# Seven products in place of eight in a feed-forward's first multiplication, with their sums on gpsimd, ScalarE and VectorE

## The chip, the cores and the metric

The kernel runs on one core of one Trainium2 chip, as one program. Its time is the device time of one execution in microseconds (us); runs are compared by their median. Engines are called as the profile calls them: PE (TensorE matmuls), PEld (its weight loads), DVE (VectorE), ACT (ScalarE), POOL (GpSimd) and SP (SyncE, which only issues DMAs here).

## What is computed

The reference runs two trunk layers over 640 tokens of width 1024: 512 latent tokens and 128 context tokens, each group with its own modulation vectors. A layer is a feed-forward, a token mixing and a second feed-forward, each behind an RMSNorm that is shifted and scaled, and each added to x with a gate:

```python
def swiglu_ffn(h, w_in, w_out):
    gate, up = jnp.split(h @ w_in, 2, axis=-1)
    return (jax.nn.silu(gate) * up) @ w_out

x = x + 0.5 * g1 * swiglu_ffn(modulate(rmsnorm(x, ...), sh1, sc1), ffn1_w_in, ffn1_w_out)
mix, ctx_state = token_mixing(modulate(rmsnorm(x, ...), sh2, sc2), ...)
x = x + g2 * mix
x = x + 0.5 * g3 * swiglu_ffn(modulate(rmsnorm(x, ...), sh3, sc3), ffn2_w_in, ffn2_w_out)
```

The hidden width is 2816, that is 22 tiles of 128. The vectors sh, sc and g are `silu(cond) @ w_ada + b_ada`, 72 tiles a layer.

## The kernel before

Tokens lie in the free dimension, features on the partitions. They are cut into half A (384 tokens) and half B (256). A feed-forward goes through its 22 hidden tiles, called units, in four blocks of 5, 5, 6 and 6 (`BLOCKS`). A unit has a gate tile and an up tile, each a sum over eight 128-feature tiles of its input. After a block's units come its out tasks: for each of eight output tiles and each half, a sum over the block's hidden tiles, added to x by `accumulate` on DVE.

Every float32 product is made of three matmuls on a high and a low part (`mm3`, lines 365 to 367), called a triple here:

```python
nc.tensor.matmul(out, hi, rhs_hi, start=start, stop=False)
nc.tensor.matmul(out, hi, rhs_lo, start=False, stop=False)
nc.tensor.matmul(out, lo, rhs_hi, start=False, stop=stop)
self.clock(MM3[rhs_hi.shape[-1]])
```

So each operand is split: ACT copies the high part (line 191) and DVE subtracts it from the source to get the low part (line 192, `split_h`). Weights come by SP's DMAs in pieces of 128x1024 and are split ahead of their use. In a unit, ACT works out silu of the gate (line 610), DVE multiplies it with the up tile out of PSUM (line 619), and the product is split into `hid`.

The order of instructions on each engine is the order in which the program is written out. A clock of the matrix work (`self.clock`, which counts the planned us of each triple) says when a piece of weight is split and when a step of background work is put in. Two kinds of background work run beside feed-forwards: `ada` (line 260), which makes modulation vectors by two 128x1024 multiply-and-sum instructions on DVE for each tile, and `ssm_build`, which makes the tables of a layer's state-space scan, in eight sets, on DVE, POOL, PE and ACT, beside each layer's first feed-forward. `ada` has 48 tiles beside the first feed-forward of layer 0 (8 of them 4.5 planned us apart, the others 7.0), 56 beside its second (8 at 4.5, then 6.5), 24 beside the first of layer 1 (10.0), and none beside the last. The first two units of the whole program are worked out beside the opening (`lead_task`).

## Time and profile before

| | us |
|---|---|
| median of 3 runs | 2525.57 |
| the runs | 2521.89 to 2526.12 |
| span of the profiled execution, first to last instruction | 2522.3 |
| PE busy | 2466.4 |
| DVE busy | 1555.2 |
| ACT busy | 812.4 |
| POOL busy | 680.9 |

The profiled execution has no time of its own beside its span; the span lies within the three runs. Busy times count instructions from their start to their end, with waits inside an instruction. Matmuls are pipelined, so the time of one matmul is longer than the distance from it to the next.

### The profile page before, as it was taken

The numbers are of one execution on the slowest core, as the hardware profiler recorded it, in microseconds if no ns is written. First come the engines' busy times: TensorE is split into PE (matmuls) and PEld (weight loads), VectorE is DVE, ScalarE is ACT, GpSimd is POOL, SyncE is SP. The second block draws the span as 40 slices with busy tenths as digits, with TensorE's granted clock in tenths as the row PEclk, the third lists the DMA queues.
The fourth block names the chain that finished last, engine by engine and source line by source line (L and its number), as shares of the span: only waits on it lengthen the run. The fifth ranks groups of instructions, "written<-read, shape, count | busy, mean of one in ns | idle before, by whom it ended". The sixth has DMA issues, their size and how long they took to land.

```text
span 2522.3 us, 44229 instructions
## 1 busy us (share of the span) xinstructions
PE 2466.4 (98%) x17428; PEld 2408.2 (95%) x17428; DVE 1555.2 (62%) x3293; ACT 812.4 (32%) x1689; POOL 680.9 (27%) x1520
## 2 busy tenths in 40 slices
PE   6999999999999999999999999999999999999999
PEld 5999999998988999999999999999998889999999
DVE  7798777557566776666568675534685764343332
ACT  5322222254444422222242222223545452222121
POOL 5105765623342000000020566551253320000000
PEclk8999999999999999999999999999999999999999
DMA  6445454325341344443324344332444212222222
GB/s 229 144 147 170 159 168 164 109 110 148 121 129 46 127 172 142 151 148 144 117 86 144 134 150 151 105 98 74 143 149 122 82 54 91 74 85 67 83 68 67
DMA packets 102115, 307.29 MB, mean 122 GB/s; under 512 B 21666, under 2 KB 24834, under 8 KB 101524
## 3 DMA queue, kind: packets, MB, share of 16 engines
q1 hardware_dynamic: 86548, 254.92, 29.8%
q0 software_dynamic: 15360, 49.56, 6.2%
q8 instruction: 137, 2.24, 0.4%
q14 instruction: 70, 0.57, 0.1%
HBM read 281.78 MB, written 23.17 MB: 121 GB/s over the span
## 4 chain that ended last, share of the span: by engine, by line
PE 87%; DVE 5%; issue 3%; ACT 2%; POOL 1%; DMA 1%; SPq 0%; DVEq 0%; POOLq 0%; ACTq 0%
PE mm L365 26%; PE mm L367 26%; PE mm L366 26%; PE mm L1389 1%; PE mm L1390 1%; PE mm L1391 1%; DVE aj L449 1%; DVE w L192 1%; PE sA L1258 1%; PE sB L1280 1%; PE mm L1227 1%; DMA T<-dT 0%; DVE H L541 0%; PE sB L1093 0%; PE sA L909 0%
## 5 line engine op out<-in xcount | busy, mean ns | idle before, releaser
L365 PE MATMUL mm<-H,w 128*128 128x384 f32 (+1 forms) x3248 | 1021.3, 314 | 9.5 <-ACT H L536 5.6
L366 PE MATMUL mm<-H,w 128*128 128x384 f32 (+1 forms) x3248 | 1011.9, 312 | 12.3 <-DVE H L541 9.3
L367 PE MATMUL mm<-H,w 128*128 128x384 f32 (+1 forms) x3248 | 1011.3, 311 | 0.0
L365 PEld LDWEIGHTS mm<-H,w 128*128 128x128 f32 x3248 | 615.0, 189 | 21.9 <-issue 13.8
L366 PEld LDWEIGHTS mm<-H,w 128*128 128x128 f32 x3248 | 615.1, 189 | 15.5 <-DVE H L541 11.1
L367 PEld LDWEIGHTS mm<-H,w 128*128 128x128 f32 x3248 | 614.7, 189 | 1.1 <-DVE w L192 1.1
L192 DVE TENSOR_TENSOR w<-r,w 128x1024 fp32r<-128x1024 f32 (+2 forms) x354 | 395.5, 1119 | 243.7 <-ACT w L191 242.3
L365 PE MATMUL mm<-hid,w 128*128 128x384 f32 (+1 forms) x1408 | 434.4, 309 | 0.0
L367 PE MATMUL mm<-hid,w 128*128 128x384 f32 (+1 forms) x1408 | 433.5, 308 | 0.0
L366 PE MATMUL mm<-hid,w 128*128 128x384 f32 (+1 forms) x1408 | 432.9, 307 | 0.0
L191 ACT ACTIVATE w<-r 128x1024 fp32r<-128x1024 f32 (+2 forms) x354 | 337.8, 956 | 289.8 <-PE mm L367 232.5
L260 DVE SCALAR_TENSOR_TENSOR aj<-ar,sbc 128x1024 bf16<-128x1024 f32 x256 | 317.4, 1240 | 36.4 <-DMA ar<-w_ada 32.4
L395 DVE SCALAR_TENSOR_TENSOR x<-mm,mod,x 128x128 f32<-128x128 f32 (+1 forms) x480 | 194.0, 434 | 183.7 <-PE mm L367 183.0
L365 PEld LDWEIGHTS mm<-hid,w 128*128 128x128 f32 x1408 | 264.1, 188 | 1.0 <-issue 1.0
L366 PEld LDWEIGHTS mm<-hid,w 128*128 128x128 f32 x1408 | 264.7, 188 | 0.0
L367 PEld LDWEIGHTS mm<-hid,w 128*128 128x128 f32 x1408 | 264.5, 188 | 0.0
L191 ACT ACTIVATE hid<-sg 128x384 fp32r<-128x384 f32 (+1 forms) x176 | 82.9, 471 | 550.4 <-DVE sg L619 534.5
L295 POOL TENSOR_TENSOR acc<-acc,sq 128x384 f32<-128x384 f32 (+1 forms) x60 | 53.7, 895 | 604.8 <-ACT sq L293 604.1
L619 DVE TENSOR_TENSOR sg<-sg,mm 128x256 f32<-128x256 f32 (+1 forms) x161 | 78.1, 485 | 212.0 <-PE mm L367 211.9
L610 ACT ACTIVATE sg<-mm 128x256 f32<-128x256 f32 (+1 forms) x161 | 70.0, 435 | 329.7 <-PE mm L367 329.7
L192 DVE TENSOR_TENSOR hid<-sg,hid 128x384 fp32r<-128x384 f32 (+1 forms) x176 | 89.2, 507 | 94.6 <-ACT hid L191 94.6
L1389 PE MATMUL mm<-w,H 128*128 128x256 f32 x480 | 143.1, 298 | 0.0
(329 smaller groups left out, 2642.2 us busy)
## 6 DMA issues: line engine op xcount, KB each, us to landing
ar<-w_ada SPq DMA_DIRECT2D x128, 512.0 KB, 4.5
r<-f1i SPq DMA_DIRECT2D x88, 512.0 KB, 3.4
r<-f0i SPq DMA_DIRECT2D x86, 512.0 KB, 3.5
r<-f0o SPq DMA_DIRECT2D x32, 384.0 KB, 3.1
r<-wqkv SPq DMA_DIRECT2D x24, 512.0 KB, 3.5
r<-f1o SPq DMA_DIRECT2D x32, 384.0 KB, 3.0
r<-f0o SPq DMA_DIRECT2D x32, 320.0 KB, 2.9
r<-f1o SPq DMA_DIRECT2D x32, 320.0 KB, 2.9
```

The lines of the kernel that those rows point to most:

```text
L191: self.nc.scalar.activation(hi, src, AF.Copy)
L192: self.nc.vector.tensor_tensor(lo, src, hi.bitcast(F32), op=ALU.subtract)
L260: nc.vector.scalar_tensor_tensor(jk, r, 1.0, self.sbc[:, c, :], op0=ALU.mult, op1=ALU.mult, accum_out=m[:, c, j * KD + k:j * KD + k + 1])
L295: eng.tensor_tensor(self.acc[X], self.acc[X], q, op=ALU.add)
L365: nc.tensor.matmul(out, hi, rhs_hi, start=start, stop=False)
L366: nc.tensor.matmul(out, hi, rhs_lo, start=False, stop=False)
L367: nc.tensor.matmul(out, lo, rhs_hi, start=False, stop=stop)
L395: nc.vector.scalar_tensor_tensor(self.x[:, m, r0:r1], p[:, r0 - s:r1 - s], self.mod[l][:, c, g * KD + m:g * KD + m + 1], self.x[:, m, r0:r ...
L449: v.scalar_tensor_tensor(jk, r, 1.0, self.sbc[:, c, :], op0=ALU.mult, op1=ALU.mult, accum_out=m[:, c, j:j + 1])
L610: nc.scalar.activation(sg[:, :e - s], p[:, :e - s], AF.Silu)
L619: nc.vector.tensor_tensor(sg[:, :e - s], sg[:, :e - s], p[:, :e - s], op=ALU.mult)
L1389: nc.tensor.matmul(p[:, :256], H[:, 0, k, ts], wh, start=k == 0, stop=False)
```

## The change

The halves are 320 tokens each. In all units but the program's first two, the products of the unit's weights with the input are taken as those of two matrices of 2 by 2 pieces: the input is cut into A and B by tokens and into its first and last four feature tiles, the weights into gate and up by columns and into the same feature halves. Seven products of such pieces, of four triples each (p1 to p7 in the code), take the place of eight. For that

- four sums of weight pieces a unit are made on POOL (`take`, 128x512 each), and seven weight pieces a unit are split instead of four pieces' worth (128x512 each; `high` on ACT, `low` on DVE);
- sums of input pieces (`x_sums`) are made once for a feed-forward, after the norm of half B, on DVE, POOL and ACT, and split;
- products that are shared are accumulated in PSUM on top of one another, and ACT copies what a bank holds midway (the prefix) to SBUF, three copies a unit;
- DVE adds or subtracts a prefix out of PSUM three times a unit, and four more combining operations of 128x320 (`tt`) go to POOL, or to DVE in the last unit of a block.

The first feed-forwards have six blocks (4, 4, 4, 4, 3, 3 units), the second ones four (6, 6, 5, 5). The out tasks and the token mixing have the same products as before. Weights are loaded in pieces of 128x512 into 24 numbered buffers, at most three sums exist at once (`NSUM`), a sum may be written out up to 13.0 planned us ahead of its use and a high part up to 9.0 (`LEAD`). Where a norm precedes, the products p1 and p2 of four units, which read half A alone, are done first (`EARLY`).

```diff
-HALF = {"A": (0, 384), "B": (384, 640)}
-RANGES = {"A": ((0, 384, 0),), "B": ((384, 512, 0), (512, 640, 1))}
-TILES = {"A": (0, 1, 2), "B": (3, 4)}
-BLOCKS = ((0, 5), (5, 5), (10, 6), (16, 6))
+HT = 320
+HALF = {"A": (0, HT), "B": (HT, 2 * HT)}
+RANGES = {"A": ((0, 320, 0),), "B": ((320, 512, 0), (512, 640, 1))}
+SEGS = {"A": ((0, 0), (128, 0), (192, 64)), "B": ((320, 0), (448, 0), (512, 64))}
+BLOCKS = (((0, 4), (4, 4), (8, 4), (12, 4), (16, 3), (19, 3)), ((0, 6), (6, 6), (12, 5), (17, 5)))
+EARLY = 4
...
-LEAD, LEAD_HOT, DMA_LAG, SPLIT_GAP = 24.0, 4.5, 3.5, 2.0
-MM3 = {384: 0.489, 256: 0.327}
+LEAD, LEAD_HOT, DMA_LAG = (13.0, 9.0), (7.0, 4.5), 3.5
+SUM_GAP, HIGH_GAP, SUM_TO_HIGH, HIGH_TO_LOW = 1.3, 0.7, 1.4, 0.6
+NW, NRAW, NSUM = 24, 7, 3
+MM3 = {320: 0.41, 256: 0.327}
...
+        def take():
+            c = order[st["a"]]
+            n, x, y = self.ops[c]
+            st["a"] += 1
+            t_sum[c] = self.T
+            if y:
+                total[c] = new((c, "t"), F32)
+                nc.gpsimd.tensor_tensor(total[c][:, :n], source(x, n), source(y, n), op=ALU.add)
+                st["sum"] = self.T
+                read(x)
...
+            if st["h"] < st["a"] and len(free) >= 2:
+                c = order[st["h"]]
+                if self.T - st["high"] >= HIGH_GAP and due(c, lead[1]) and \
+                        self.T - t_sum[c] >= (SUM_TO_HIGH if self.ops[c][2] else 0.0):
+                    high()
+            if st["a"] < len(order):
+                c = order[st["a"]]
+                if due(c, lead[0]) and (not self.ops[c][2] or
+                                        self.T - st["sum"] >= SUM_GAP and len(total) < NSUM and len(free) > 2) and \
+                        all(x is None or x[0] == "o" or x[1] in raw and self.T - when[x[1]] >= DMA_LAG
+                            for x in self.ops[c][1:]):
+                    take()
...
+    def x_sums(self, k, r12, r22):
...
+        v.tensor_tensor(t1, h11, r12, op=ALU.subtract)
+        g.tensor_tensor(t3, r12, r22, op=ALU.subtract)
+        v.tensor_tensor(t1, t1, l11, op=ALU.add)
+        v.tensor_tensor(t2, r22, t1, op=ALU.add)
+        g.tensor_tensor(t4, h21, t2, op=ALU.subtract)
+        g.tensor_tensor(t4, t4, l21, op=ALU.add)
...
+        def high(u, X, src):
+            hid[u, X] = [new((u, X, i), F32R) for i in range(2)]
+            nc.scalar.activation(hid[u, X][0], tmp[src], AF.Copy)
+        def low(u, X, src):
+            a, b = hid[u, X]
+            v.tensor_tensor(b, tmp[src], a.bitcast(F32), op=ALU.subtract)
+            drop(src)
...
+        def p1(w, u):
+            bank["a", u] = self.ps()[:, :HT]
+            self.product(bank["a", u], w, "11", True)
+            nc.scalar.activation(temp((u, "p")), bank["a", u], AF.Copy)
+        def p2(w, u):
+            p = bank.pop(("a", u))
+            self.product(p, w, "21", False)
+            nc.scalar.activation(temp((u, "a")), p, AF.Silu)
+        def p5(w, u):
+            bank["c", u] = self.ps()[:, :HT]
+            self.product(bank["c", u], w, "t1", True)
+            nc.scalar.activation(temp((u, "c")), bank["c", u], AF.Copy)
+        def p6(w, u):
+            bank["b", u] = self.ps()[:, :HT]
+            self.product(bank["b", u], w, "t2", True)
+            nc.scalar.activation(temp((u, "b")), bank["b", u], AF.Copy)
+        def steps(gap, *fns):
+            for n, fn in enumerate(fns):
+                self.later(gap * (n + 1), fn)
+        def tt(u, out, a, b, op):
+            (v if u in ends else nc.gpsimd).tensor_tensor(out, a, b, op=op)
+        def p3(w, u):
+            p = bank.pop(("c", u))
+            self.product(p, w, "22", False)
+            s, sg = temp((u, "s")), tmp[u, "b"]
+            v.tensor_tensor(s, p, tmp[u, "p"], op=ALU.add)
+            def gate():
+                tt(u, sg, s, sg, ALU.subtract)
+                drop((u, "s"))
+            steps(2 - (u in ends), gate, lambda: nc.scalar.activation(sg, sg, AF.Silu))
+        def p7(w, u):
+            self.product(bank["b", u], w, "t3", False)
+            s, a, b = temp((u, "s")), tmp[u, "b"], tmp[u, "c"]
+            v.tensor_tensor(s, bank["b", u], tmp[u, "p"], op=ALU.subtract)
+            def sub():
+                tt(u, b, s, b, ALU.subtract)
+                drop((u, "s"))
+            def mult():
+                tt(u, b, a, b, ALU.mult)
+                drop((u, "b"))
+            steps(2 - (u in ends), sub, mult, lambda: high(u, "B", (u, "c")), lambda: low(u, "B", (u, "c")))
+        def p4(w, u):
+            p = bank.pop(("b", u))
+            self.product(p, w, "t4", False)
+            a, b = tmp[u, "a"], tmp[u, "p"]
+            v.tensor_tensor(b, p, b, op=ALU.subtract)
+            def mult():
+                tt(u, b, a, b, ALU.mult)
+                drop((u, "a"))
+            if u in ends:
+                mult()
+                high(u, "A", (u, "p"))
+                self.later(2, lambda: low(u, "A", (u, "p")))
+            else:
+                steps(2, mult, lambda: high(u, "A", (u, "p")), lambda: low(u, "A", (u, "p")))
...
+        def units(us, early):
+            for u in early[:3], early[3:]:
+                if u:
+                    items.extend(early_task(u))
+            for n, u in enumerate(us):
+                if u not in early:
+                    items.append(task(p1, u, "11"))
+                items.append(task(p5, u, "s1"))
+                if n:
+                    items.append(task(p4, us[n - 1], "22"))
+                items.append(task(p6, u, "s2"))
+                if u not in early:
+                    items.append(task(p2, u, "12"))
+                items.append(task(p3, u, "s4"))
+                items.append(task(p7, u, "s3"))
+            items.append(task(p4, us[-1], "22"))
...
+            self.ops[op("s1")] = (512, r["p0"], r["p1"])
+            self.ops[op("s2")] = (512, ("o", op("s1")), r["g0"])
+            self.ops[op("s4")] = (512, ("o", op("s2")), r["g1"])
+            self.ops[op("s3")] = (512, r["g0"], r["p0"])
...
+            if lead and b == 0:
+                items.append(lead_task(us[:2]))
+                items += lead_rest(us[1])
+                items.append(("call", lambda: self.norms.update(B=self.spawn(self.all_x_sums(), 0.0, True))))
+                units(us[2:], us[2:])
+            else:
+                units(us, us[:n_early] if b == 0 else [])
```

What this does to DVE's queue in a middle unit of the last feed-forward: before, six rows are one unit (L192 of `w` is the low part of a weight piece, L619 the product with the up tile, L192 of `hid` the low part of the unit's result, for half A and half B).

```order
L192 TENSOR_TENSOR w_25880<-r_25762,w_25880 128x1024
L192 TENSOR_TENSOR w_25912<-r_25794,w_25912 128x1024
L619 TENSOR_TENSOR sg_25894<-sg_25894,mm_25896 128x384
L192 TENSOR_TENSOR hid_25742<-sg_25894,hid_25742 128x384
L619 TENSOR_TENSOR sg_25954<-sg_25954,mm_25956 128x256
L192 TENSOR_TENSOR hid_25808<-sg_25954,hid_25808 128x256
```

Of the change, the twelve rows of one unit on DVE (L220 is the low part of a weight piece, L889, L900 and L916 combine a PSUM bank, `mm`, with a prefix, L852 is the low part of a result).

```order
L220 TENSOR_TENSOR w_31032<-w_30978,w_31031 128x512
L220 TENSOR_TENSOR w_31051<-w_30751,w_31050 128x512
L852 TENSOR_TENSOR hid_31057<-hid_30837,hid_31056 128x320
L220 TENSOR_TENSOR w_31077<-w_31023,w_31076 128x512
L889 TENSOR_TENSOR hid_31106<-mm_30996,hid_30994 128x320
L220 TENSOR_TENSOR w_31101<-w_30933,w_31100 128x512
L900 TENSOR_TENSOR hid_31128<-mm_31038,hid_30994 128x320
L220 TENSOR_TENSOR w_31122<-w_31067,w_31121 128x512
L220 TENSOR_TENSOR w_31143<-w_31088,w_31142 128x512
L852 TENSOR_TENSOR hid_31160<-hid_31017,hid_31159 128x320
L220 TENSOR_TENSOR w_31166<-w_30908,w_31165 128x512
L916 TENSOR_TENSOR hid_30994<-mm_31038,hid_30994 128x320
```

The two long rows on weights have become seven of half the width, and the two products three with PSUM. POOL has nothing to do in the units of the last feed-forward of the kernel before; of the change, these eight rows on POOL belong to one unit of the last feed-forward (L199 adds two weight pieces, L883 is a combining operation).

```order
L199 TENSOR_TENSOR w_30910<-w_30866,w_30776 128x512
L199 TENSOR_TENSOR w_30931<-w_30621,w_30641 128x512
L883 TENSOR_TENSOR hid_30902<-hid_30949,hid_30902 128x320
L199 TENSOR_TENSOR w_30978<-w_30798,w_30908 128x512
L883 TENSOR_TENSOR hid_30860<-hid_30971,hid_30860 128x320
L883 TENSOR_TENSOR hid_30860<-hid_30902,hid_30860 128x320
L199 TENSOR_TENSOR w_31023<-w_30978,w_30778 128x512
L883 TENSOR_TENSOR hid_30837<-hid_30925,hid_30837 128x320
```

POOL thus has eight instructions a unit, each with two operands in SBUF, mixed from two chains. In layer 0's first feed-forward, a set of the scan's tables begins on POOL before with six rows one after the other (`EP` and `tp` are parts of a table).

```order
L728 TENSOR_TENSOR EP_2247<-Bb_2215,PW_1570 128x256
L729 TENSOR_TENSOR tp_2217<-Bb_2215,PW_1570 128x256
L730 TENSOR_TENSOR EP_2247<-EP_2247,tp_2217 128x256
L731 TENSOR_TENSOR tp_2217<-Bb_2215,PW_1570 128x256
L732 TENSOR_TENSOR EP_2247<-Bb_2215,PW_1570 128x256
L736 TENSOR_TENSOR EP_2247<-EP_2247,tp_2217 128x256
```

Of the change, rows of the same kind stand between weight sums and combining operations of the units, in one queue.

```order
L199 TENSOR_TENSOR w_4110<-w_4050,w_3946 128x512
L1107 TENSOR_TENSOR EP_4090<-EP_4090,tp_4057 128x256
L1108 TENSOR_TENSOR tp_4057<-Bb_4055,PW_1920 128x256
L199 TENSOR_TENSOR w_4137<-w_3743,w_3771 128x512
L1110 TENSOR_TENSOR EP_4090<-Bb_4055,PW_1920 128x256
L1111 TENSOR_TENSOR EP_4090<-EP_4090,tp_4057 128x256
L883 TENSOR_TENSOR hid_4102<-hid_4155,hid_4102 128x320
L199 TENSOR_TENSOR w_4186<-w_3975,w_4108 128x512
L883 TENSOR_TENSOR hid_4044<-hid_4179,hid_4044 128x320
L883 TENSOR_TENSOR hid_4044<-hid_4102,hid_4044 128x320
L199 TENSOR_TENSOR w_4242<-w_4186,w_3948 128x512
```

## Rows read from the trace of the kernel before

**Rows 1.** The page: busy totals, and 40 slices of DVE and POOL in tenths.

```profile
PE 2466.4 (98%) x17428; PEld 2408.2 (95%) x17428; DVE 1555.2 (62%) x3293; ACT 812.4 (32%) x1689; POOL 680.9 (27%) x1520
...
DVE  7798777557566776666568675534685764343332
...
POOL 5105765623342000000020566551253320000000
```

**Rows 2.** The page: chain of waits that ended last, by engine.

```profile
PE 87%; DVE 5%; issue 3%; ACT 2%; POOL 1%; DMA 1%; SPq 0%; DVEq 0%; POOLq 0%; ACTq 0%
```

**Rows 3.** Timeline of PE in a unit: start us, us, engine, line, tile, shape.

```profile
299.84 0.28 PE L366 MATMUL mm<-H,w 128*128 128x256 f32 x1
...
301.85 0.34 PE L365 MATMUL mm<-H,w 128*128 128x384 f32 x1
...
308.55 0.34 PE L367 MATMUL mm<-H,w 128*128 128x384 f32 x1
```

**Rows 4.** Groups by line and shape: count | busy us, mean ns | idle before.

```profile
L260 DVE SCALAR_TENSOR_TENSOR aj<-ar,sbc 128x1024 bf16<-128x1024 f32 x256 | 317.4, 1240 | 36.4 <-DMA ar<-w_ada 32.4 <-ACT sbc L252 2.7
...
L192 DVE TENSOR_TENSOR w<-r,w 128x640 fp32r<-128x640 f32 x64 | 53.5, 836 | 34.8 <-ACT w L191 34.2
...
L192 DVE TENSOR_TENSOR hid<-sg,hid 128x384 fp32r<-128x384 f32 x88 | 50.1, 569 | 52.1 <-ACT hid L191 52.1
L191 ACT ACTIVATE w<-r 128x640 fp32r<-128x640 f32 x64 | 46.6, 729 | 30.4 <-PE mm L367 30.4
L191 ACT ACTIVATE hid<-sg 128x384 fp32r<-128x384 f32 x88 | 46.2, 525 | 300.6 <-DVE sg L619 296.0 <-DVE sg L634 4.5
...
L192 DVE TENSOR_TENSOR hid<-sg,hid 128x256 fp32r<-128x256 f32 x88 | 39.1, 444 | 42.6 <-ACT hid L191 42.6
...
L295 POOL TENSOR_TENSOR acc<-acc,sq 128x384 f32<-128x384 f32 x30 | 30.5, 1016 | 538.2 <-ACT sq L293 538.0
...
L295 POOL TENSOR_TENSOR acc<-acc,sq 128x256 f32<-128x256 f32 x30 | 23.3, 775 | 66.6 <-ACT sq L293 66.1
```

**Rows 5.** Timeline: POOL alone at 216 us; DVE and POOL at 450 us.

```profile
216.33 0.21 POOL L728 TENSOR_TENSOR T<-T 128x14 f32<-128x14 f32 x1
...
450.30 1.22 DVE L192 TENSOR_TENSOR w<-r,w 128x1024 fp32r<-128x1024 f32 x1
...
450.40 0.19 PEld L367 LDWEIGHTS mm<-H,w 128*128 128x128 f32 x1
```

**Rows 6.** Timeline at 304.8 us, DVE and POOL.

```profile
304.77 0.73 POOL L730 TENSOR_TENSOR EP<-EP,tp 128x256 f32<-128x256 f32 x1
304.78 1.81 DVE L192 TENSOR_TENSOR w<-r,w 128x1024 fp32r<-128x1024 f32 x1
...
305.58 1.49 POOL L731 TENSOR_TENSOR tp<-Bb,PW 128x256 f32<-128x256 f32 x1
```

**Rows 7.** Timeline at 1661.6 us: POOL beside a DVE instruction that reads PSUM.

```profile
1661.60 0.83 POOL L736 TENSOR_TENSOR EP<-EP,tp 128x256 f32<-128x256 f32 x1
...
1661.76 0.54 DVE L619 TENSOR_TENSOR sg<-sg,mm 128x384 f32<-128x384 f32 x1
```

**Rows 8.** Windows: length, busy us (instructions) of each engine, PE clock, DMA share.

```profile
200.00:500.00 300.00, 300.00 (x2082) 296.60 (x2081) 219.42 (x394) 75.59 (x127) 198.57 (x505) 1.00 0.47 156
1400.00:1700.00 300.00, 300.00 (x2074) 296.58 (x2074) 177.99 (x328) 74.34 (x122) 175.68 (x502) 1.00 0.38 127
2250.00:2300.00 50.00, 50.00 (x338) 50.00 (x337) 17.89 (x28) 11.00 (x16) 0.00 (x0) 1.00 0.23 81
1250.00:1300.00 50.00, 48.96 (x333) 48.47 (x332) 27.54 (x67) 18.33 (x33) 13.84 (x15) 1.00 0.26 95
2050.00:2100.00 50.00, 48.24 (x314) 47.72 (x313) 29.18 (x68) 24.43 (x51) 5.86 (x7) 0.97 0.21 72
575.00:580.00 5.00, 2.63 (x16) 2.27 (x14) 0.57 (x1) 1.66 (x4) 0.00 (x0) 1.00 0.48 187
580.00:585.00 5.00, 4.75 (x37) 4.47 (x38) 4.83 (x14) 2.94 (x8) 0.00 (x0) 0.71 0.57 171
```

More of the change, by code (lines that the diff above doesn't have):

```diff
@@ L104, in run @@
                     last[c] = i
-        W = self.NW
-        raws, tiles, when = {}, {}, {}
-        st = {"d": 0, "s": 0, "x": 0, "i": 0, "t": self.T}
+        place = {c: j for j, c in enumerate(order)}
+        rorder, users, sums = [], {}, {}
+        for c in order:
+            for x in self.ops[c][1:]:
+                if x and x[0] == "r":
+                    if x[1] not in users:
+                        users[x[1]] = 0
+                        rorder.append(x[1])
+                    users[x[1]] += 1
+                elif x:
+                    sums.setdefault(x[1], []).append(c)
@@ new lines, in read, with over @@
+        def read(x):
+            if x[0] == "r":
+                users[x[1]] -= 1
+                if not users[x[1]]:
+                    raw.pop(x[1])
+                    free.append(slot.pop(x[1]))
+                    dma()
+        def over(c):
+            if c in total and place[c] < st["l"] and all(place[d] < st["a"] for d in sums.get(c, ())):
+                total.pop(c)
+                free.append(slot.pop((c, "t")))
+                dma()
+        def take():
[8 more added lines that the diff above has]
+                read(x)
+                read(y)
+                if x[0] == "o":
+                    over(x[1])
@@ new lines, in high, with low @@
+        def high():
+            c = order[st["h"]]
+            n, x, y = self.ops[c]
+            src = source(("o", c) if y else x, n)
+            pair[c] = new((c, 0), F32R), new((c, 1), F32R)
+            nc.scalar.activation(pair[c][0][:, :n], src, AF.Copy)
+            t_high[c] = st["high"] = self.T
+            st["h"] += 1
+        def low():
+            c = order[st["l"]]
+            n, x, y = self.ops[c]
+            src = source(("o", c) if y else x, n)
+            hi, lo = pair[c]
+            nc.vector.tensor_tensor(lo[:, :n], src, hi[:, :n].bitcast(F32), op=ALU.subtract)
+            st["l"] += 1
+            if y:
+                over(c)
+            else:
+                read(x)
@@ new lines, in due, with splitter @@
+        def due(c, lead):
+            return begin[first[c]] - (self.T - t0) <= lead
+        def splitter():
+            if self.dlimit is not None:
+                return
+            lead = LEAD_HOT if self.hot else LEAD
+            if st["l"] < st["h"] and self.T - t_high[order[st["l"]]] >= HIGH_TO_LOW:
+                low()
+            if st["h"] < st["a"] and len(free) >= 2:
+                c = order[st["h"]]
+                if self.T - st["high"] >= HIGH_GAP and due(c, lead[1]) and \
[8 more added lines that the diff above has]
+                    take()
@@ L142, in run, with have @@
+        def have(ops):
+            dma()
+            while any(place[c] >= st["l"] for c in ops):
+                if st["l"] < st["h"]:
+                    low()
+                elif st["h"] < st["a"]:
+                    high()
+                else:
+                    take()
+            return [pair[c] for c in ops]
+        self.dma, self.splitter, self.get = dma, splitter, have
         for i, it in enumerate(items):
-            st["i"] = i
             if it[0] == "call":
@@ L558, in opening @@
             if k:
[L559 to L560 removed]
+                low(k)
+            yield k, w
         assert not todo and next(by_pool, "end") == "end"
```

671 lines of the change are left out of this document (390 added, 281 removed).

## The prediction

> **What bounds the kernel now.** I read the page's totals first, then the chain of waits, then stretches. PE is busy for 98% of the span [rows 1], and 87% of the chain that ended last is PE [rows 2], so only fewer or shorter matmuls, or a new wait of PE, move the end. The timeline of PE gives the price: 17 matmuls of 256 tokens take 301.85 - 299.84 = 2.01 us, 0.118 each, and 38 of 384 tokens take 308.55 - 301.85 = 6.70 us, 0.176 each [rows 3], so 0.46 ns a token, 0.147 us for 320 and 0.442 for a triple. POOL is idle for whole slices and DVE is busy 62% [rows 1]; both look like room for the sums. What matters is whether the room of the two is one room, and that takes the timelines below.
>
> **What it removes.** Each of 86 units has 28 triples for 32, so 344 x 0.442 = 152 us less of PE. In all, a unit falls from 32 x 0.442 = 14.14 us to 28 x 0.442 = 12.37; the out tasks (22 x 16 x 0.442 = 156 us a feed-forward) stay. The profiled span of 2522.3 would become 2370 if nothing else moved. The median of the runs lies 3.3 us above that span, which I add at the end.
>
> **What it adds on ACT and elsewhere.** From [rows 4], ACT's copy of 640 columns takes 729 ns and of 384 takes 525, hence 627 for 512 and about 470 for 320. A unit has seven of the first and seven of the second kind (three prefixes, two silus, two high parts): 7.7 us of 12.37, beside PE. DVE's extra gated adds (two more blocks in each first feed-forward) fall into out tasks, where nothing else is dense. Twice as many DMAs of half the size carry about the same bytes, at a DMA share near 0.23 to 0.47 [rows 8]. I cost these at nothing; the cover is PE's own time, and it goes if ACT has to wait for a sum or a combining operation of POOL, since ACT's queue is in order and the next prefix copy stands behind.
>
> **What it adds on POOL and DVE: one room, not two.** At 450.30 us DVE starts a low part of 1024 columns, two operands in SBUF, 1.22 us long. POOL's instruction of 14 columns starts 0.10 later and lasts 1.19 where it takes 0.21 alone [rows 5]: it got through from 450.40 + 1.19 - 0.21 = 451.38 on. DVE kept it out for 1.08 us, its own duration less 0.14. The other way, at 304.77, POOL's 0.73 us instruction is under way, DVE's low part starts 0.01 later and lasts 1.81, 0.59 too long, and POOL's next one in turn lasts 1.49 [rows 6]: POOL kept DVE out for its duration less 0.13. A DVE instruction with PSUM as one operand ran at its 0.54 us beside POOL [rows 7]. So sums and combining operations on POOL, and low parts and `ada` on DVE, take turns, and their turns add up.
>
> The turns of a middle unit: POOL's add takes 1016 ns at 384 columns and 775 at 256 [rows 4], by the line 1257 at 512 and 896 at 320; less 0.13, four of 1.13 and four of 0.77 are 7.6 us. DVE's low part takes 836 ns at 640, 569 at 384 and 444 at 256 [rows 4], so 702 at 512 and 507 at 320; less 0.14, seven of 0.56 and two of 0.37 are 4.66. Sum 12.26 us, against PE's 12.37: full, with nothing beside it. Beside `ada`, each tile is two turns of 1.24 - 0.14, and 1.08 by [rows 5], so 2.16 us; a unit is 28 x 0.41 = 11.48 planned us, hence 1.64 tiles at a pace of 7.0, 1.77 at 6.5, 1.15 at 10.0: the unit's turns become 15.8, 16.1 and 14.7 us. A set of the scan's tables: POOL is busy 198.6 us with 505 instructions for eight sets [rows 8], 24.8 a set, waits and DMA issues in it. Less 505 x 0.13 that is 16.6; by a small one's share (0.08 of 0.21, [rows 5]) it is 9.4. I take 14, DVE's part in it, between the two. Eight sets beside the last 14 units of a first feed-forward and their out tasks (14 x 12.37 + 14 x 7.07 = 272 us, 173 of it units) put 0.36 of a set beside a unit, 5.1 us (3.4 by the low bound).
>
> What of that reaches PE: weights are split 9.0 planned us ahead, 9.7 real (0.442 for 0.41). A block loses its units times (turns - 12.37) less that lead, and the out tasks, in which POOL rests, bring the lead back. Turns never follow one another without a gap, since either queue also waits for data; [rows 6] shows a hand-over without any, so I add 5%, near that end.
> - First feed-forward, layer 0: the second block 4 x (16.6 - 12.37) - 9.7 = 7; the next two, with tables, 4 x (21.9 - 12.37) - 9.7 = 28 each; then 3 units 19, and 8 without `ada`; 10 for the input sums at the start (below). Sum 100.
> - Second, layer 0: 6 x (16.9 - 12.37) - 9.7 = 17.5, twice, 13 twice for five units, and 5 for the first eight tiles' faster pace. Sum 66.
> - First, layer 1 (`ada` ends about two thirds through): 3, 3, 24, 24, 8, 8. Sum 70.
> - Second, layer 1: 6 x 0.5 = 3, within the lead. Sum 0.
> - Starts of the last three: before, PE is idle 1 to 2 us there [rows 8]. Four input sums, each four turns on POOL (0.77) and six on DVE (0.37), are 21 us, to be done before p5 and p6 can end, with the norm of half B ahead of them; p1 and p2 of four units give PE 32 x 0.442 = 14. I take 9 each, 27 (bounds 13 and 40).
>
> Sum 263 us against 152 saved: 2522.3 - 152 + 263 + 3.3 = 2637. With no gaps, tables at 3.4 a unit and starts at 13, the same sums give 60 + 48 + 27 + 13 = 148, so 2522.
>
> The Trainium skill, "SBUF — State Buffer", section "Who interferes with whom", states that a DVE instruction with two SBUF inputs and a GpSimd instruction that reads SBUF exclude each other for the whole instruction, and that the other fully blocks. On the exclusion the trace agrees; taken with whole durations, which these rows shorten by 0.13 to 0.14 us, the rule gives 2826 us, the second rival below, in place of 2637.
>
> **The rivals.**
> *The turns fit (faster).* If POOL and DVE use the out tasks for the units' work, only a whole feed-forward's turns count: units, out weights' low parts (24 us), input sums (21), `ada`, tables (9.4 a set) against PE's 428 us (410 for layer 0's first, without its lead units). Layer 0 first: 245 + 24 + 23 + 104 + 75 = 471, 61 over; layer 0 second 270 + 24 + 21 + 121 = 436, 8 over; layer 1 first 270 + 24 + 21 + 52 + 75 = 442, 14 over; the last none. With 13 for starts, 2522.3 - 152 + 96 + 3.3 = 2470. For it speaks that DVE is at 18 of 50 us without `ada` and POOL at 0 [rows 8]; against it, that the queues are in order and at most three sums exist. It decides from a lead of about 25 us instead of 9.7.
> *Each instruction keeps the other out for its whole duration (much slower).* A unit's turns are then 4 x 1257 + 4 x 896 + 7 x 702 + 2 x 507 ns = 14.5 us, 18.6 to 18.9 beside `ada`, and a table set 19.8, 7.1 a unit. The same sums give 160 + 110 + 134 + 8 + 40 = 452, so 2826. Towards it also works that PE, after idling 2.4 of 5 us at 575, had a granted clock of 0.71 in the next 5 us [rows 8]: each stall may cost a second time. Against it speak [rows 5, 6].
> *No change to measure.* The low bound, 2522, lies there, but only by a balance of unlike sizes.
>
> **How the numbers follow.** My forecast (2531 to 2725) has 0.57, the turns that fit 0.21, whole durations or worse 0.19, a balance within 0.2% (5 us, about what a measurement of this kernel can tell) 0.03. Faster 0.21, same 0.03, slower 0.76. The range reaches to the first rival's 2455, of whose spread down to PE's bound (2400) it leaves out a third, and to 2750 towards the second, which leaves out two thirds of that one: about 0.8 inside. The forecast's own range is 2531 to 2725.
>
> **What would show it.** Right: PE's matmuls of the units keep 0.147 us, and PE gets waits for DVE's low parts (`w`) or ACT's copies that were absent; POOL's adds of 512 columns last well above 1.26 us in the mean, and DVE's low parts above 0.70; the units of layer 1's second feed-forward pass at about 12.4 us, those beside `ada` at 15 or more. Wrong: PE busy at 98% again with a span near 2400, or waits of PE that end with PE's own PSUM banks or with DMAs.

## The result, and the profile after

The changed kernel takes 2969.55 us in the median of four runs, 2525.03 before: 1.176 times as long, with a 95% interval of 1.174 to 1.178. Slower was forecast, but at 2637 us, with a range that ended at 2750. The profiled execution has a span of 2960.9 us at a mean granted clock of 0.921 (2522.3 at 0.992 before). All that follows goes by that span, so 438.6 us more where the forecast had 111 (263 less 152): 328 short.

The page's busy times, and its slices for three engines and the clock, against [rows 1]:

```profile
PE 2493.5 (84%) x16420; PEld 2388.6 (81%) x16420; DVE 2239.4 (76%) x4224; ACT 1120.6 (38%) x2613; POOL 1576.2 (53%) x2192
...
PE   6678788785999958898986888879889997899999
...
DVE  7899778865656688989886887877757576757766
...
POOL 5434777776334373636344557787753434734632
PEclk8899889897999979999997999989989998899999
```

PE is no longer the engine that is always busy, and no other engine is busy all the time either: DVE 76%, POOL 53%. Two engines that are half and three quarters busy can still be the limit if they work in turns. The chain of waits accounts for too little of this span to be of use, so the next view is PE's waits, by whom it waited for (us in all, times, longest us):

```profile
PE mm L582 <- ACT hid L876: 114.3, 48, 5.7
PE mm L582 <- DVE hid L900: 113.7, 58, 6.2
PE mm L582 <- ACT hx L544: 66.1, 12, 7.4
PE mm L582 <- ACT hid L941: 25.0, 5, 14.0
PE mm L582 <- ACT hid L871: 24.6, 13, 4.3
PE mm L582 <- DVE x L620: 23.1, 11, 7.8
PE mm L582 <- ACT hx L496: 21.3, 2, 18.1
```

L876 is ACT's copy of the prefix out of bank b (in `p6`), L900 DVE's subtraction that reads the same bank (in `p7`), L544 ACT's copy of a sum of input halves (in `x_sums`), L496 the first tiles of a norm at the start of a mixing. So PE does not wait for weights (DVE's low parts account for 1.8 us here), but for its own PSUM banks to be read, and for the sums of the input. Of the prediction's signs, ACT's late copies are one of those named for right, and waits for PE's own PSUM banks one of those named for wrong; both came.

Why they are read late is in the means of the groups by shape (count, then busy us and mean ns, then idle time before). [rows 4] had 1240 ns for `ada`; on lines through the sizes there, a low part came to 702 ns for 512 columns and 507 for 320, and POOL's add to 1257 and 896:

```profile
L220 DVE TENSOR_TENSOR w<-w 128x512 fp32r<-128x512 f32 x778 | 720.5, 939 | 183.7 <-ACT w L211 121.3 <-POOL w L199 41.1 <-issue 11.1
L386 DVE SCALAR_TENSOR_TENSOR aj<-ar,sbc 128x1024 bf16<-128x1024 f32 x256 | 381.6, 1491 | 8.3 <-DMA ar<-w_ada 5.7 <-ACT sbc L378 2.3
...
L852 DVE TENSOR_TENSOR hid<-hid 128x320 fp32r<-128x320 f32 x176 | 138.8, 789 | 125.1 <-ACT hid L848 124.6
...
L900 DVE TENSOR_TENSOR hid<-mm,hid 128x320 f32<-128x320 f32 x86 | 41.5, 482 | 9.4 <-PE mm L584 9.4
...
L199 POOL TENSOR_TENSOR w<-w 128x512 f32<-128x512 f32 x344 | 529.0, 1541 | 415.3 <-PE mm L583 217.1 <-DVE w L220 99.1 <-issue 48.2
L883 POOL TENSOR_TENSOR hid<-hid 128x320 f32<-128x320 f32 x264 | 311.7, 1181 | 223.6 <-DVE hid L916 103.4 <-DVE hid L889 88.8 <-DVE hid L900 19.9
```

Each of these with two operands in SBUF, on either engine, is a fifth to a half longer than by those rows (low parts 0.94 us for 0.70 and 0.79 for 0.51, `ada` 1.49 for 1.24, POOL 1.54 for 1.26 and 1.18 for 0.90). The one with an operand in PSUM (L900) is not stretched: its 86 lie between 0.475 and 0.495 us.

By stage the view of windows shows where it happens (the first feed-forward and the mixing with the second, for each layer; columns: stretch, its us, then busy us of PE, PE's weight loads, DVE, ACT and POOL, PE's granted clock, DMA share, GB/s):

```profile
0.00:706.00 706.00, 536.26 (x3142) 513.69 (x3142) 564.59 (x1013) 224.69 (x475) 432.27 (x647) 0.87 0.36 119
706.00:1573.00 867.00, 745.64 (x5135) 710.95 (x5134) 682.60 (x1300) 346.02 (x855) 391.63 (x457) 0.94 0.37 117
1573.00:2186.00 613.00, 492.71 (x3021) 472.30 (x3020) 464.14 (x868) 211.03 (x447) 418.24 (x698) 0.90 0.31 97
2186.00:2961.00 775.00, 718.87 (x5128) 691.64 (x5126) 528.03 (x1047) 338.88 (x836) 334.07 (x392) 0.96 0.29 91
```

In the trace of before the same stages are these, so they grow by 172, 112, 135 and 20 us:

```profile
0.00:534.50 534.50, 506.91 (x3384) 497.55 (x3384) 401.32 (x774) 162.13 (x291) 253.83 (x551) 0.98 0.46 157
534.50:1290.10 755.60, 743.51 (x5387) 720.94 (x5386) 496.80 (x1070) 263.15 (x596) 118.40 (x226) 0.99 0.38 130
1290.10:1768.20 478.10, 477.06 (x3285) 473.10 (x3284) 295.69 (x631) 137.29 (x235) 200.60 (x532) 1.00 0.36 121
1768.20:2522.30 754.10, 738.95 (x5374) 716.61 (x5374) 361.43 (x818) 249.84 (x573) 108.04 (x214) 0.99 0.28 90
```

Three stretches of units show the three cases, beside `ada` alone, beside `ada` and tables, and beside neither:

```profile
1340.00:1421.00 81.00, 67.58 (x423) 65.61 (x422) 75.43 (x100) 31.00 (x69) 47.73 (x32) 0.94 0.39 127
300.00:389.00 89.00, 65.09 (x348) 61.55 (x348) 62.07 (x95) 26.35 (x57) 72.08 (x120) 0.82 0.37 115
2759.00:2822.00 63.00, 61.56 (x417) 60.86 (x416) 51.77 (x61) 30.17 (x66) 40.41 (x32) 1.00 0.27 81
```

DVE is in an instruction for 75 of 81 us where `ada` runs, POOL for 72 of 89 where the tables run, because the time that an instruction is kept out counts as its own; only the third is PE's. In the second block of layer 0's second feed-forward (1199.8 to 1298.1) one of the two is in an instruction for 98.6% of the time, and PE for 83%. Timing each block's units from the last matmul of the out tasks before to the first of its own, a unit takes, after a feed-forward's first block, 20.5 us (layer 0, first feed-forward), 16.2 (second), 18.4 (layer 1, first) and 12.8 (second).

The start of layer 0's second feed-forward, 1022 to 1068, holds one more pattern. The timeline of DVE, POOL and ACT between 1052 and 1060 (a line's x3 is three instructions merged):

```profile
1052.01 0.48 DVE L533 TENSOR_TENSOR xt<-hx,xn 128x320 f32<-128x320 f32 x1
1052.52 0.49 DVE L535 TENSOR_TENSOR xt<-xt,hx 128x320 f32<-128x320 f32 x1
1053.04 0.49 DVE L536 TENSOR_TENSOR xt<-xn,xt 128x320 f32<-128x320 f32 x1
...
1053.54 1.57 DVE L549 TENSOR_TENSOR hx<-xt,hx 128x320 fp32r<-128x320 f32 x2
1053.61 1.15 POOL L537 TENSOR_TENSOR xt<-hx,xt 128x320 f32<-128x320 f32 x1 [1.88 <-DVE xt L536]
1054.84 0.99 POOL L538 TENSOR_TENSOR xt<-xt,hx 128x320 f32<-128x320 f32 x1
1055.79 0.86 POOL L552 TENSOR_TENSOR hx<-xt,hx 128x320 fp32r<-128x320 f32 x1
1055.86 0.47 ACT L544 ACTIVATE hx<-xt 128x320 fp32r<-128x320 f32 x1 [1.47 <-POOL xt L538]
...
1056.36 0.63 DVE L554 TENSOR_TENSOR hx<-xt,hx 128x320 fp32r<-128x320 f32 x1 [1.25 <-ACT hx L544]
1056.92 0.66 DVE L492 SCALAR_TENSOR_TENSOR xn<-x,mod,sB 128x192 f32<-128x192 f32 x2
...
1059.38 0.48 DVE L533 TENSOR_TENSOR xt<-hx,xn 128x320 f32<-128x320 f32 x1
```

One tile's sums of inputs go DVE, POOL, ACT, DVE, and the next tile starts only behind DVE's last instruction of this one: 59.38 - 52.01 = 7.37 us from tile to tile. Of these, 56.36 + 0.63 - 52.01 = 4.98 us are the sums; in the rest the norm makes the next tile (L492 and what follows it). PE's last product with a plain half of the input ended near 1037.7, when the first of the four tiles was just out; the other three stand in the open, as the window on them shows (7 us of PE in 26, and at the lower of the clock's two levels for most of it):

```profile
1038.00:1064.00 26.00, 6.97 (x19) 4.92 (x20) 18.70 (x31) 13.28 (x32) 16.85 (x17) 0.57 0.05 14
```

### The profile page after: what moved, and what is told of

Read it like the earlier page. It is cut to its first block, busy times and chain, and to the rows that moved or that the text cites. A ratio compares the mean times of both kernels' runs of the same rounds, so it can differ in the third digit from the quotient of the medians.

```text
span 2960.9 us, 46450 instructions
## 1 busy us (share of the span) xinstructions
PE 2493.5 (84%) x16420; PEld 2388.6 (81%) x16420; DVE 2239.4 (76%) x4224; ACT 1120.6 (38%) x2613; POOL 1576.2 (53%) x2192
## 5 line engine op out<-in xcount | busy, mean ns | idle before, releaser
L582 PE MATMUL mm<-hx,w 128*128 128x320 f32 x2904 | 979.0, 337 | 380.4 <-ACT hid L876 114.3
L583 PE MATMUL mm<-hx,w 128*128 128x320 f32 x2904 | 954.6, 329 | 15.6 <-DVE hx L759 11.0
L220 DVE TENSOR_TENSOR w<-w 128x512 fp32r<-128x512 f32 (+2 forms) x938 | 812.2, 880 | 189.1 <-ACT w L211 126.1
L584 PE MATMUL mm<-hx,w 128*128 128x320 f32 x2904 | 950.4, 327 | 1.9 <-DVE w L220 1.8
L582 PEld LDWEIGHTS mm<-hx,w 128*128 128x128 f32 x2904 | 593.0, 204 | 432.4 <-DVE hid L900 129.7
L211 ACT ACTIVATE w<-w 128x512 fp32r<-128x512 f32 (+2 forms) x938 | 542.1, 601 | 601.7 <-POOL w L199 201.1
L199 POOL TENSOR_TENSOR w<-w 128x512 f32<-128x512 f32 x344 | 529.0, 1541 | 415.3 <-PE mm L583 217.1
L583 PEld LDWEIGHTS mm<-hx,w 128*128 128x128 f32 x2904 | 593.5, 204 | 22.5 <-DVE hx L759 12.5
L584 PEld LDWEIGHTS mm<-hx,w 128*128 128x128 f32 x2904 | 593.3, 204 | 2.8 <-DVE w L220 2.7
L582 PE MATMUL mm<-hid,w 128*128 128x320 f32 x1408 | 440.1, 313 | 13.7 <-DVE x L620 13.3
L583 PE MATMUL mm<-hid,w 128*128 128x320 f32 x1408 | 437.3, 311 | 0.3
L584 PE MATMUL mm<-hid,w 128*128 128x320 f32 x1408 | 436.9, 310 | 0.0
L883 POOL TENSOR_TENSOR hid<-hid 128x320 f32<-128x320 f32 x264 | 311.7, 1181 | 223.6 <-DVE hid L916 103.4
L386 DVE SCALAR_TENSOR_TENSOR aj<-ar,sbc 128x1024 bf16<-128x1024 f32 x256 | 381.6, 1491 | 8.3 <-DMA ar<-w_ada 5.7
L620 DVE SCALAR_TENSOR_TENSOR x<-mm,mod,x 128x192 f32<-128x192 f32 (+1 forms) x576 | 232.5, 433 | 140.6 <-PE mm L584 139.4
L582 PEld LDWEIGHTS mm<-hid,w 128*128 128x128 f32 x1408 | 267.7, 190 | 17.3 <-issue 10.8
L852 DVE TENSOR_TENSOR hid<-hid 128x320 fp32r<-128x320 f32 x176 | 138.8, 789 | 125.1 <-ACT hid L848 124.6
L1765 PE MATMUL mm<-w,hx 128*128 128x256 f32 x480 | 142.9, 298 | 0.0
L1767 PE MATMUL mm<-w,hx 128*128 128x256 f32 x480 | 136.6, 285 | 0.0
```

Source lines behind the costliest of these rows:

```text
L199: nc.gpsimd.tensor_tensor(total[c][:, :n], source(x, n), source(y, n), op=ALU.add)
L211: nc.scalar.activation(pair[c][0][:, :n], src, AF.Copy)
L220: nc.vector.tensor_tensor(lo[:, :n], src, hi[:, :n].bitcast(F32), op=ALU.subtract)
L386: nc.vector.scalar_tensor_tensor(jk, r, 1.0, self.sbc[:, c, :], op0=ALU.mult, op1=ALU.mult, accum_out=m[:, c, j * KD + k:j * KD + k + 1])
L582: nc.tensor.matmul(out, hi, rhs_hi, start=start, stop=False, skip_group_check=parts)
L583: nc.tensor.matmul(out, hi, rhs_lo, start=False, stop=False, skip_group_check=parts)
```

## The experiments

Each is one run with a profile beside a run of the kernel before (2523.8 to 2526.9 us). The changed kernel's profiled execution took 2963.0 us, and small differences below are between spans. The theory from the trace: the sum of the turns that POOL and DVE take from each other sets the units, and the chain of input sums the starts. Its first rival: the order in ACT's queue, where PE's copies stand behind a silu that waits for POOL.

**Combining operations on VectorE.** In `tt`:

```
-            (v if u in ends else nc.gpsimd).tensor_tensor(out, a, b, op=op)
+            v.tensor_tensor(out, a, b, op=op)
```

> Only move: the four combining operations of a middle unit run on VectorE instead of gpsimd. Theory of the turns (gpsimd and VectorE exclude each other where both operands are in SBUF, and a middle unit is as long as the sum of its turns): four turns of 0.77 us become four of 0.37, so a unit that waits loses 1.6 us; 52 units beside ada or the tables wait, 83 us, and the last feed-forward, near its limit, some 5; with some clock back about 2860 us (2840 to 2885), and units beside ada fall from 16.2 to about 14.6 us. Rival, order of the queues (PE waits because ScalarE's copies out of PSUM stand behind a silu that waits for gpsimd, whatever the number of turns): that wait goes, units beside ada fall to about 13 us, and the time to 2700 to 2780 us.

2882.5 us. Units by feed-forward 18.8, 15.5, 16.5 and 12.5 us (20.5, 16.2, 18.4, 12.8). Inside 2840 to 2885, far from the rival's 2780: POOL out of ACT's chain helped no more than its shorter turns say. Beside `ada` it helped less: 0.7 us of an expected 1.6.

**No sums of weights.** In `ffn_items`, for each of the four:

```
-            self.ops[op("s1")] = (512, r["p0"], r["p1"])
+            self.ops[op("s1")] = (512, r["p0"], None)
```

> Left out: the four sums of weights of a unit (gpsimd's 512-column instructions); the products take plain pieces of the weights in their place, with the same splits. Theory of the turns: a unit's turns fall from 12.26 to 7.7 us, and with 1.77 tiles of ada to 11.6, under PE's 12.4; so layer 0's second feed-forward passes at 12.5 to 13 us a unit instead of 16.2, only units beside the tables stay long (16 to 17), the starts stay; with the clock about 2760 us (2720 to 2800). Rival, order of the queues: gpsimd's combining operations and the waits behind them remain, a unit beside ada stays above 14.5 us, and the time above 2840 us.

2717.2 us; units 16.4, 13.4, 15.2, 12.5. Just under the theory's 2720; the rival's 14.5 beside `ada` did not come.

**`ada` in 16 of 1024 columns.**

```
...
-    nc.vector.scalar_tensor_tensor(jk, r, 1.0, self.sbc[:, c, :], ...
+    nc.vector.scalar_tensor_tensor(jk[:, :16], r[:, :16], 1.0, self.sbc[:, c, :16], ...
```

> Changed: each of ada's VectorE instructions takes 16 of 1024 columns (the rest of its product is left out); its DMAs, its pace and the number of instructions stay. Theory of the turns: 1.8 tiles a unit cost 2 x 1.1 us each; without them layer 0's second feed-forward passes at 12.8 us a unit, as layer 1's second does with no ada (63 us in four stretches, 18 more in its first block), units beside ada and tables lose 2 to 3.5 us each; with the clock about 2800 us (2770 to 2830). Rival, order of the queues: ada is in VectorE's queue alone and ScalarE's copies stay late; no more than 60 us less, above 2900 us.

2795.4 us; units 17.5, 13.0, 17.3, 12.8. Layer 0's second feed-forward passes like layer 1's, as the turns have it: an instruction that is in VectorE's queue alone had made it 3.2 us a unit longer.

**No sums of inputs.** `x_sums` emits nothing, and `p5`, `p6`, `p7`, `p4` read the operand "11" for "t1" to "t4".

> Left out: the sums of input halves at the start of each feed-forward, with their splits (11 to 13 instructions a tile, four tiles); the four products that read them read the first plain half. Theory now held of the starts: the sums come after the norm of the second half, when PE has used up the plain products, and as one chain of 7.37 us a tile, so nothing hides their 29 us; without them PE's lump of 25 to 28 us idle goes in three starts, about 20 go in the opening, and some clock: 2840 us (2815 to 2865). Rival, the step of the forecast (a start costs 9 us, the rest of the excess is in the units): 4 x 9 less, about 2925 us.

2881.3 us, 16 over the theory's range and 44 under the time that the forecast's step gave. The units stay (20.6, 16.2, 18.2, 12.8); the four stretches up to the first out task lose 20, 20, 20 and 14 us. So these sums cost 74 us, under half of what the starts cost (next section). Four times 4.98 us is 20 us, the loss of three of the four stretches; the 29 that I had expected are four times 7.37, with the norm's part in them.

**Everything on VectorE.** The edit of the first experiment, and in `take`:

```
-                nc.gpsimd.tensor_tensor(total[c][:, :n], source(x, n), source(y, n), op=ALU.add)
+                nc.vector.tensor_tensor(total[c][:, :n], source(x, n), source(y, n), op=ALU.add)
```

> The changed kernel with a unit's four sums of weights and its four combining operations all on VectorE; gpsimd keeps the tables and its parts of norms and inputs. Theory of the turns: with gpsimd silent, VectorE's low part of 512 columns is back at 0.68 to 0.72 us in the mean in both second feed-forwards (0.94 over the changed kernel), a unit is 10.6 us of VectorE's own queue, 14.7 beside ada, so 12.4 in layer 1's second and 14.5 to 15 in layer 0's: about 2850 us (2830 to 2875). Rival, the low part is slow for another reason (its reads of weights just written by ScalarE or by DMAs): its mean stays above 0.85 us.

2740.1 us (span 2738.3, 223 less), with eight more instructions a unit on the engine that was the busier one. That is 110 us under the 2850 expected, which names only the second feed-forwards; the units of the first ones fell by about 4 us each too. Its groups of DVE by shape:

```profile
L220 DVE TENSOR_TENSOR w<-w 128x512 fp32r<-128x512 f32 x778 | 542.9, 704 | 72.4 <-ACT w L211 70.3
L386 DVE SCALAR_TENSOR_TENSOR aj<-ar,sbc 128x1024 bf16<-128x1024 f32 x256 | 316.8, 1238 | 7.7 <-DMA ar<-w_ada 5.1 <-ACT sbc L378 2.3
L199 DVE TENSOR_TENSOR w<-w 128x512 f32<-128x512 f32 x344 | 242.3, 704 | 0.0
```

The same 778 low parts take 704 ns in place of 939, and the same 256 `ada` instructions 1238 in place of 1491. What had made them long was POOL's work beside them. The reads of fresh weights, the rival, are the same in both runs. Units 16.3, 14.1, 14.7, 12.5.

**Lead, longer and shorter.** Two runs of the changed kernel; first `LEAD` (18.0, 14.0) for (13.0, 9.0) with `NRAW, NSUM` 5, 4 for 7, 3, then `LEAD` (7.0, 4.5).

> The changed kernel with weights split 14.0 planned us ahead of use in place of 9.0, sums 18.0 ahead in place of 13.0 and four sums at a time in place of three (five plain pieces in flight in place of seven, for room). The forecast took one lead off the excess of every block. Theory now: PE waits for results of PSUM banks, that VectorE's and gpsimd's full queues deliver late, and not for weights, so a longer lead takes nothing off: 2961 us within 15. Rival, the forecast's step: 5 planned us more lead, 5.4 real, off each of 17 blocks, some 90 us less, 2870 us or under.

> The changed kernel with the lead halved: weights 4.5 planned us ahead in place of 9.0, sums 7.0 in place of 13.0. Theory: where turns are the limit a lead is used up at once, so little changes in the units beside ada or tables; the last feed-forward, which just fits, may lose its slack: 2961 to 3000 us. Rival, the lead hides part of each block's excess as forecast: 4.9 us back on each of 17 blocks, 80 us, 3040 us or more.

2958.9 and 3007.9 us (spans 3.8 less and 45.2 more). With the longer lead one to four more weight pieces lie split when a block's first out task begins, and it hides nothing more. Less costs 45, between the two expectations, and the rows of PE's waits show that now it is weights that come late, as they did not before (L220 is DVE's low part, L211 ACT's high part):

```profile
PE mm L584 <- DVE w L220: 95.7, 102, 4.3
PE mm L582 <- ACT w L211: 74.2, 51, 4.2
```

**PE's eighth product given back.** In `p5`, the product is made twice into the same bank:

```
-            self.product(bank["c", u], w, "t1", True)
+            for _ in range(2):
+                self.product(bank["c", u], w, "t1", True)
```

> The changed kernel, each unit's first product with a sum of inputs made twice into the same bank (the second restarts it), so that PE does eight products a unit, 152 us more at full clock, and nothing else changes. Theory: turns of VectorE and gpsimd and the sums of inputs set the time, PE waits anyway, and with more work it keeps its clock in more places; only the 22 units of layer 1's second feed-forward, which PE nearly fills, grow by 1.3 us: 2990 us (2965 to 3020). Rival, PE's own time at the low clock sets the units: 152 us or more on top, 3110 us.

3041.9 us (span 79 more, clock 0.930): neither. Of 1.77 us a unit, 1.6, 0.7, 1.3 and 1.4 reach the time (units 22.1, 16.9, 19.7, 14.2). So PE's time is not simply hidden behind the turns. An explanation would be the loop through bank b, in which `p7` goes on only when the copy of `p6`'s result is out, so that PE, ACT and DVE are in series for part of a unit; it was not tried by itself. What the low clock costs by itself this run does not settle, since the clock moved little.

**The tables' end.** `ssm_build` waits 3.0 and 0.3 planned us where it waited 8.0 and 3.0.

> The changed kernel with one edit: the scan's tables wait 7.7 planned us less a set. Theory: 20 to 27 us of PE waiting at the start of layer 0's mixing are the last set of the tables, drained behind the feed-forward; they go, units beside the tables get at most a part back as denser turns: 2945 us (2930 to 2958). Rival, the wait there is the norm's own chain, or the denser turns cost as much: 2965 us or more.

2962.5 us (span 0.7 less): no change. The wait moved as expected: the stretches around the start of layer 0's mixing lose 10 us in the last out tasks and 13 behind them, where PE's wait for the norm's first tiles (L496) fell from 18.1 us to 1.9. The units beside the tables took it all back (20.7 and 19.1 us, the worst block 23.8 for 22.4). That was the rival, and it is what turns that only add up should do; I had expected only a part back.

**Eight products in the new frame.** The other six runs ask what is left without the seven products. A `MODE` for each feed-forward chooses how a unit is made; "8" makes gate and up of each half from two products into one bank, with the second half's first part where "t3" was:

```
...
+                    for h in range(2):
+                        self.product(p, w[h], PLAIN[mode][X][h], h == 0)
+                    unit_done([u], X)(n, p)
...
```

> Undone: the seven products; all four feed-forwards take eight, without sums of weights, inputs or results, and all else of the change stays (halves of 320 tokens, weights in pieces of 512 columns, blocks of three to six units). Theory of the turns: without the sums nothing excludes VectorE for long, PE's work is that of the kernel before (2343 us at full clock), so 2515 to 2545 us. Rival, the new frame costs by itself (twice as many small instructions and DMAs, two more blocks): above 2580 us.

2591.7 us: the rival's case, that the frame costs by itself. The units stand at PE's own 14.1 to 14.4 us in all four, so the frame has no part in the long units. But 68 us over the kernel before are the frame's: by stages, 43 in the stretches up to the first out task, the rest around out tasks; there PE waits for norms and, up to 7.8 us at once, for a sum of squares; the last table set is written from 513 to 556 us (468 to 501 before), right up to the mixing.

For the next, only layer 1's second is "7", with the combining on VectorE:

> Eight products as in the run beside it in three feed-forwards, seven in layer 1's second alone, where neither ada nor tables run; combining operations on VectorE. Theory of the turns with exposed starts: 22 units at 12.5 in place of 14.1 us give 36 us, the one start, with its sums of inputs behind the norm, costs 40 to 45: 2530 us (2520 to 2550). Rival, seven products lose in the units wherever they run: 2570 us or more.

2590.8 us, by its number the rival's case, and 0.9 less than the run beside it: some 35 us won in 22 units, nearly all of it lost at the one start. That is as the theory had it (36 won, 40 to 45 lost); the base was higher by the frame.

Then the first block of that one is four plain units, and the sums start behind two of them:

```
...
+                            self.drain(self.norms["B"])
+                            self.sum_gap = 6.0
+                            self.norms["B"] = self.spawn(self.all_x_sums(), 1.0)
...
```

> As the run before, but the first four units of layer 1's second feed-forward take eight products, for which the second half's first part is kept beside the sums, and the sums of inputs are made during these units. Theory: the chain of 7.4 us a tile is hidden behind PE's 56 us of plain units, nothing of the start is left, 18 units save 1.65 us each, 30 us: 2495 us (2485 to 2512), faster than the kernel before. Rival, the sums cost by the turns that they take wherever they stand: 10 us or more come back, above 2515 us.

2570.3 us, 21 less than with eight products throughout, though on the frame's higher base it is not the 2495 expected and not under the kernel before. With the input sums made during plain units, seven products do gain, where nothing else takes turns; the 30 us expected came to 21, since PE still has 7.8 us idle where the sevens begin.

The last three: the same in layer 0's second, with `ada`'s pace by place; then the run above with another order in `norm` and the tables' waits as above; then both, with 13.0 and 4.6 for the paces:

```
...
-                    yield pace / 4 if c == 0 else pace * 3 / 4
+                    pc = pace if not self.phase or j == 8 else 3.5 if self.phase == "out" else 25.0
+                    yield pc / 4 if c == 0 else pc * 3 / 4
...
-        ks = (0, 4, 1, 5, 2, 6, 3, 7) if plain and X == "B" else range(KD)
+        ks = (0, 4, 1, 5, 2, 6, 3, 7) if plain and X == "B" and mode == "7" else range(KD)
```

> As the run before, and the same in layer 0's second feed-forward, with ada paced by place: a tile each 25 planned us beside units of seven products, each 3.5 in the out tasks, where gpsimd rests. Theory of the turns: a seven-product unit has 10.7 us of turns with the combining on VectorE, 0.5 tile of ada adds 1.0, so it fits in 12.4; another 30 us are saved: 2466 us (2452 to 2490). Rival, ada beside the out tasks holds up their results (VectorE is needed for each) or units still pass at 14 us: above 2495 us.

> From the run with eight products in three feed-forwards and the sums behind four plain units in the last (2570 us): the second half's norm makes its tiles in the order in which eight products read them, and the scan's tables wait 7.7 planned us less a set, so that the last set ends before the feed-forward does. Theory: of the 68 us that eight products in the new frame lost, some 30 are PE waiting for the last set at the start of the mixing and some 20 the start of three feed-forwards: 2530 us (2515 to 2548). Rival, denser tables take their turns from the units: 2560 us or more.

> The run beside it, with layer 0's second feed-forward in seven products as well (four plain units ahead) and ada at a tile each 13 planned us beside such units and each 4.6 in the out tasks, so that it ends in time: 48 tiles in 18 units and the out tasks. Theory of the turns: 10.7 + 0.9 x 2.16 = 12.6 us a unit in place of 14.1, 18 units, 26 us less than the run beside it, about 2505 us (2490 to 2525). Rival, ada beside out tasks delays them as much as it frees the units: no more than 5 us apart.

The first gave 2601.3, the second 2556.6, the third 2594.5 us: past the rival's bound, between the two, and 38 us above the run beside it. Order and tables gave back 14 of the frame's 68 us, with 16.4 us a unit in one block beside denser tables; 54 stay open. Seven products beside `ada` lose at both paces: the times are 31 and 38 us above the runs without them. The units came to 13.6 to 14.3 us where I had 11.7 and 12.6, so they saved next to nothing against the 14.1 of eight products. The loss itself lies elsewhere: some 26 us ahead of the second block, in both runs, and in the last out tasks, which take 66 and 60 us in place of 42. There the rest of `ada` stands close together ahead of the next norm, for which PE waits 17 and 11 us. No version was faster than the kernel before.

## Why the prediction fell short, step by step

- *PE loses 152 us.* Right as far as PE goes: beside neither `ada` nor tables a unit falls to 12.8 us, 12.5 with the combining on VectorE, against 12.37.
- *POOL and DVE exclude each other, less 0.13 to 0.14 us.* Right; the run with everything on VectorE shows the exclusion. The 0.14 was read from this row of POOL, beside DVE's row at 450.30 in [rows 5]:

```profile
450.40 1.19 POOL L732 TENSOR_TENSOR T<-T 128x14 f32<-128x14 f32 x1
```

  The Trainium skill, "SBUF — State Buffer", "Who interferes with whom", gives the exclusion; the runs agree on it (939 against 704 ns). Its rule with whole durations was worth 18.6 to 18.9 us a unit beside `ada`; measured are 16.2, nearer to the forecast's 16.9.
- *The turns of a unit.* Right in size. The forecast's units, after each first block, are 20.1, 16.9, 18.8 and 12.9 us; measured 20.5, 16.2, 18.4 and 12.8. Times their numbers (18, 16, 18, 16) over 12.37 that is an excess of 336 forecast and 323 measured. The tables' share was a choice between two bounds and the gaps a flat 5%, so a match this close is in part luck. Nor is a unit the sum of the turns alone: 1.77 us more of PE made it 0.7 to 1.6 longer.
- *"A block loses its units times (turns - 12.37) less that lead."* This step failed. It took 9.7 us from each of 13 blocks and 8 more in the last feed-forward, so of the 336 the forecast kept 200. None of it was hidden: 323 were lost, **123 us short**. Lead covers weights, and PE waits for its PSUM banks instead, where no work is stored ahead; with a longer lead the time was the same.
- *"I take 9 each" for the starts.* This step failed too, and with it the cover that it counts on. From the end of the feed-forward ahead of it (so with the mixing, where one lies between) up to its first out task, a feed-forward's stretch is 39.7, 86.8, 53.3 and 51.2 us longer than before, corrected for the units in it (14.14 each) and 1.77 saved by each unit of seven; 231 in all. The forecast had 10, 31.5, 12 and 9, 62.5: **168 us short**. The reason given, that p1 and p2 of four units (14 us) cover the sums, was wrong: they read the first half and were used up under the norm of the second, by the time of the first sum. Of the 231, 74 are the input sums (left out, they go). By the units' own means about 66 are turns of the units in first blocks, and 43 appear with eight products in the new frame. The rest, 48, is not told apart in full. Layer 0's mixing holds part of it: ahead of the feed-forward's first unit it is 20.7 us longer than before (2.7 with eight products), and 12.7 of these went when the tables ended earlier. The clock, 0.70 in the stretch 1022 to 1068, is another candidate.
- *The frame at nothing.* Wrong: 68 us, 43 of them within the starts. Out tasks and changes of block cost the remaining **37 us** of the shortfall (323 + 231 + 37 - 152 = 439).
- *ACT at nothing.* ACT is idle for 62%, but its copy (L876) is PE's longest wait. With everything on VectorE that group falls from 114.3 to 46.8 us without an edit on ACT, so ACT was late, not full.
- *The clock* stood in a rival alone. The lower level of the clock (1.2 GHz) was granted for 470 us (44 before), which by a count of the matmuls in those windows is an estimated 121 us more of PE's matmul time. Most of it lies where PE had waited just before, so part would have been waiting anyway; how much is its own is open.

The rival with the better time, "the turns fit", fell with the lead: out tasks lend nothing to units, because no queue holds a unit's results ahead.

## What to carry to other kernels

Before work is moved to an idle GpSimd, ask which operands it reads: with two in SBUF on either side, its time and VectorE's add up, and the slower engine keeps the other out for longer (the shortest of the 344 adds of 512 columns took 1.26 us, VectorE alone 0.70), so the busier VectorE can be the better place. Take a lead off a stall only if what is late is what the lead stores; for each wait, name the buffer and ask how far ahead it can be filled. And at the start of a stage, list what cover is still unused when the new work can begin, not how much there is in all.

## What the runs showed of the hardware that was not expected

Giving the busier engine eight more instructions a unit made the whole faster by 223 us (spans 2960.9 and 2738.3), and the mean of its unchanged instructions fell by 25% (939 to 704 ns) and 17% (1491 to 1238). Tables that were made denser cost as much in the units (worst block 23.8 us a unit for 22.4) as they freed behind them. And 152 us more of matmuls moved the mean clock only from 0.921 to 0.930 and the time by half of their length, 79 us, though PE was idle for 16% of the span.
